# The second half's output projection as seven half-size block products, with the row scales moved into the left factors

## The chip, the cores and the metric

One core of a Trainium2 chip runs the kernel. The metric is the device time of one execution in microseconds (us). Everything is float32; a product is made of three fast passes, by splitting each operand into a high and a low part (high x high, high x low, low x high).

## What is computed

```python
proj = einsum('bld,de->ble', rms_norm(x, norm_w), w_in)        # 2048 tokens, 2048 -> 4608
q, k, v, z_attn, u, z_ssm = split(proj, ...)
o_attn = swa_sink_attention(q, k, v, positions, ...) * silu(z_attn)    # 1024 wide
y = gelu(s5_ssm(u, ...))
y = y * sigmoid(y @ w_glu + b_glu)
o_ssm = y * silu(z_ssm)                                          # 1024 wide
merged = concatenate([rms_norm(o_attn, attn_out_norm_w), rms_norm(o_ssm, ssm_out_norm_w)])
out = x + einsum('ble,ed->bld', merged, w_out)                   # 2048 -> 2048
```

## The kernel before, in words

The 2048 tokens go in two halves of 1024. What one stage leaves for another goes through buffers in HBM (OA for the attention's output, YS for the ssm's, ZS and ZA for the gates). A list scheduler orders the instructions of each engine from the program's order and from priorities; steps of a side task get a priority 800 instructions ahead of their place. Each engine, and SyncE's queue (SP), which issues the DMAs, then works through its own queue in that order.

At the end of the program stand three stages. First the *panels* of the first half's output: `out_panel` makes 256 columns for 1024 tokens with the two row groups of `w_out` one after the other (i = 0, 1). Each group takes 192 matmuls of `panel_tok` (L343) into four PSUM banks (psg, of which there are four), 384 a panel. As a group ends, VectorE (DVE) scales it by row and adds it into four tiles xr that hold x. `weave` runs seven of these panels beside `attend_all`, the second half's attention: 16 groups of four heads and two query blocks, 64 *pairs* of two heads and one block. A pair is four score matmuls (L516), a masked softmax on DVE and ScalarE (ACT), two transposes (L541), the split of the probabilities (ph, pl), their masking (pm: the high part on GpSimd (POOL), the low part on DVE) and four value matmuls (L556). `self.stage` hands out the 512 KB staging tiles (pool stg, four buffers, tag "s"): the four xr of a panel are such tiles, and so is whatever else is loaded for a while.

Then `glu`: eight panels of `panel_feat` (L325) for the gated unit, with `tail_attn` as its side task. It loads the attention rows (oa, a staging tile), splits them with the gain into mh/ml (`split`), and sums their squares into acca; `row_scale` makes the row factors ra from it. At its end the ssm rows yg are split too, and rss is made.

Last `out_wide`: the second half's output, 512 columns at a time over all eight banks, 2 x 8 weight tiles of 128x512 for each. `w_unit` loads a tile (wr), ACT copies it to wh, DVE makes wl = wr - wh, and 24 matmuls (L979) use it. Three buffers each hold wr, wh and wl. The row factors ra and rss come in as the banks are emptied.

## Time and profile before

| | before |
|---|---|
| three runs | 2889.68, 2891.08, 2891.10 us (median 2891.08) |
| profiled execution, its span | 2892.7 us |
| granted TensorE clock, mean | 0.992 |
| TensorE (PE) busy | 2813.6 us, 97% |
| DVE busy | 1900.9 us, 66% |
| ACT busy | 968.2 us, 33% |
| POOL busy | 201.0 us, 7% |

The span runs from the first to the last instruction of one profiled execution. PE is the engine to watch: what another engine does costs time only where PE waits for it. A share over the whole span mixes stages with different limits, so the rows further down are taken by stretches of time.

### The profile page before, as it was taken

Reading aid. Unit: us, or ns where it says so; the run is one execution under the profiler, and the core shown is the slowest. Engines: PE = TensorE matmul, PEld = TensorE weight load, DVE = VectorE, ACT = ScalarE, POOL = GpSimd, SP = SyncE. Lnnn points to the kernel's source line nnn. Section 1 sums busy time; section 2 is a strip of 40 time slices with the busy share of each in tenths; the row PEclk is TensorE's granted clock in tenths of the full one; section 3 lists DMA queues with packets and bytes.
Section 4 is the critical chain, followed back from the end, with each engine's and each line's share of the span. In section 5 each row is a group of like instructions: output and inputs, shape, how many; then the busy total and the mean of one; then the engine's idle time right before and its main releaser. Section 6 shows DMA issues by size and latency. Waiting matters only on the chain.

```text
span 2892.7 us, 45678 instructions
## 1 busy us (share of the span) xinstructions
PE 2813.6 (97%) x17123; PEld 2515.5 (87%) x17123; DVE 1900.9 (66%) x4479; ACT 968.2 (33%) x2117; POOL 201.0 (7%) x341
## 2 busy tenths in 40 slices
PE   6899999989999999999999999998999999899999
PEld 5789999878888888888999988878999999778887
DVE  6681746856773776677779985378999875842222
ACT  6421212133442444333323332255444433521110
POOL 0000000001110021100000000000222220000000
PEclk9999999999999999999999999999999999999999
DMA  5842526553332533445455554343444436333321
GB/s 175 226 123 63 164 88 172 142 141 106 99 113 76 177 108 97 128 145 146 146 160 151 149 154 141 116 125 95 144 135 124 125 111 189 99 101 107 106 78 58
DMA packets 430541, 369.09 MB, mean 128 GB/s; under 512 B 56560, under 2 KB 388848, under 8 KB 430320
## 3 DMA queue, kind: packets, MB, share of 16 engines
q1 hardware_dynamic: 428256, 366.16, 42.6%
q8 instruction: 135, 2.21, 0.3%
q14 instruction: 86, 0.70, 0.1%
q10 hardware_dynamic: 2064, 0.01, 0.0%
HBM read 270.74 MB, written 99.55 MB: 128 GB/s over the span
## 4 chain that ended last, share of the span: by engine, by line
PE 81%; DVE 8%; DMA 7%; SPq 2%; ACT 1%; issue 1%; POOL 0%; ACTq 0%; POOLq 0%; DVEq 0%
PE psg L325 32%; PE psg L343 28%; PE psg L979 6%; PE pss L979 3%; DMA oa<-OA 2%; PE pss L516 2%; PE pso L556 2%; PE pso L979 1%; PE pst L979 1%; DVE ml L93 1%; DMA xst<-in_x_dram 1%; DVE yg L84 1%; PE pst L541 1%; DMA TCS<-St 1%; PE pss L810 1%
## 5 line engine op out<-in xcount | busy, mean ns | idle before, releaser
L84 DVE TENSOR_TENSOR wl<-wr,wh 128x512 fp32r<-128x512 f32 x456 | 315.4, 692 | 544.2 <-ACT wh L311 534.7
L311 ACT CAST wh<-wr 128x512 fp32r<-128x512 f32 x456 | 283.2, 622 | 1007.8 <-PE psg L325 330.9
L325 PE MATMUL psg<-xh,wl 128*128 128x512 f32 x1536 | 495.0, 394 | 7.2 <-DVE wl L84 7.2
L325 PE MATMUL psg<-xl,wh 128*128 128x512 f32 x1536 | 498.4, 395 | 0.0
L325 PE MATMUL psg<-xh,wh 128*128 128x512 f32 x1536 | 493.9, 395 | 0.5 <-ACT xh L235 0.5
L343 PE MATMUL psg<-wl,xh 128*128 128x256 f32 x1536 | 435.2, 284 | 0.0
L343 PE MATMUL psg<-wh,xh 128*128 128x256 f32 x1536 | 434.2, 284 | 1.0 <-ACT rx L389 1.0
L343 PE MATMUL psg<-wh,xl 128*128 128x256 f32 x1536 | 434.2, 284 | 0.0
L325 PEld LDWEIGHTS psg<-xh,wl 128*128 128x128 f32 x1536 | 287.8, 189 | 65.2 <-DVE wl L84 8.9
L325 PEld LDWEIGHTS psg<-xh,wh 128*128 128x128 f32 x1536 | 287.0, 189 | 57.2 <-ACT xh L235 0.9
L325 PEld LDWEIGHTS psg<-xl,wh 128*128 128x128 f32 x1536 | 288.1, 189 | 55.8
L343 PE MATMUL psg<-wh,mh 128*128 128x256 f32 x1024 | 289.9, 286 | 8.6 <-ACT tt L927 7.8
L343 PEld LDWEIGHTS psg<-wh,xh 128*128 128x128 f32 x1536 | 293.6, 192 | 1.4 <-ACT rx L389 1.2
L343 PEld LDWEIGHTS psg<-wl,xh 128*128 128x128 f32 x1536 | 294.2, 192 | 0.4 <-DVE wl L84 0.2
L343 PEld LDWEIGHTS psg<-wh,xl 128*128 128x128 f32 x1536 | 293.7, 192 | 0.0
L343 PE MATMUL psg<-wl,mh 128*128 128x256 f32 x1024 | 290.2, 285 | 0.6 <-DVE wl L84 0.6
L343 PE MATMUL psg<-wh,ml 128*128 128x256 f32 x1024 | 288.9, 285 | 0.0
L84 POOL TENSOR_TENSOR pm<-ph,sel 128x256 fp32r<-128x256 f32 x240 | 189.5, 811 | 983.1 <-ACT ph L544 647.2
L343 PEld LDWEIGHTS psg<-wh,mh 128*128 128x128 f32 x1024 | 195.1, 192 | 9.4 <-ACT tt L927 8.0
L343 PEld LDWEIGHTS psg<-wl,mh 128*128 128x128 f32 x1024 | 196.4, 192 | 0.8 <-DVE wl L84 0.8
L343 PEld LDWEIGHTS psg<-wh,ml 128*128 128x128 f32 x1024 | 195.4, 192 | 0.0
L533 ACT ACTIVATE sm<-pss,mx,rs 128x128 f32<-128x128 f32 x240 | 108.6, 459 | 96.3 <-DVE mx L93 90.5
(419 smaller groups left out, 4663.0 us busy)
## 6 DMA issues: line engine op xcount, KB each, us to landing
wr<-in_w_in_dram SPq DMA_DIRECT2D x296, 256.0 KB
wr<-in_w_out_dram SPq DMA_DIRECT2D x128, 256.0 KB
tb<-TCS SPq DMA_DIRECT2D x64, 256.0 KB
xr<-in_x_dram SPq DMA_DIRECT2D x64, 256.0 KB
out_dram<-xr SPq DMA_DIRECT2D x64, 256.0 KB
raw<-MBC SPq DMA_DIRECT2D x32, 384.0 KB
kst<-KK SPq DMA_DIRECT2D x56, 192.0 KB
xst<-in_x_dram SPq DMA_DIRECT2D x16, 512.0 KB
```

What stands on the lines that cost most here:

```text
L84: (eng or self.nc.vector).tensor_tensor(out=out, in0=a, in1=b, op=op)
L93: self.nc.vector.scalar_tensor_tensor(out=out, in0=a, scalar=s, in1=b, op0=op0, op1=op1)
L311: nc.scalar.copy(hi, raw)
L325: nc.tensor.matmul(ps[t], wt[:, kk, :], xx[k][:, t * 512:(t + 1) * 512], start=(k == 0 and i == 0), stop=(k == nkc - 1 and i == 2))
L343: nc.tensor.matmul(o, xx[k][:, sl], wt[:, kk, :], start=(k == 0 and i == 0 and t % 2 == 0), stop=(k == nkc - 1 and i == 2), skip_group_che ...
L516: nc.tensor.matmul(ps[:, h * 256:h * 256 + 256], qst[:, bq % 2, hp * 2 + h, :], kst[:, i, ksl], start=(h == 0 and i == 0), stop=(i == 1), ...
L533: nc.scalar.activation(sm[:, h, :], sc[:, h, :], AF.Exp, scale=rs[:, h:h + 1], bias=negm[:, h:h + 1], accum_out=den[:, h:h + 1])
L541: nc.tensor.transpose(pt[:, h * P:(h + 1) * P], sm[:, h, :], self.ident)
L556: nc.tensor.matmul(po, vst[:, blk + kb, :], pm[:, i, kb], start=(i == 0 and kb == 0), stop=(i == 1 and kb == 1))
L810: nc.tensor.matmul(o, m[:, g, 0:128], u[:, g, 384:640], start=(g == 0 and i == 0), stop=(i == 2), skip_group_check=True)
L979: nc.tensor.matmul(ps[t], xx[k0 + k][:, t * P:(t + 1) * P], wt[:, 0, :], start=(k == 0 and j == 0), stop=(k == 7 and j == 2))
```

## The change

The second half's projection Y = A W is cut into 2 x 2 blocks: A by tokens (2 x 512) and by rows (attention, ssm), W by rows and by columns (B11, B12, B21, B22 of 1024 x 1024). Instead of eight block products it makes seven, of sums and differences of the blocks (Strassen). The row factors can't then wait for the eviction: `spread` turns ra and rss into full tiles rba and rbs, and the left factors are scaled before they are combined. The attention's sum of squares is made earlier, as nine more steps behind the attention's 33 in the weave with the panels (`attn_stats`, in place of that part of `tail_attn`). The left factors stand in three slots (fh, fl) and are formed by side tasks: slots 0 and 1 beside the gated unit (`form_first`), the others each beside an earlier product. Combinations of weight blocks are made on POOL from two loaded tiles; two of them (T3, T2) are also stored to HBM for a later product. A product is two column halves of eight steps; a step is one weight tile and 12 matmuls into four banks. `final` adds x and a base on POOL and the bank on DVE.

```diff
+    def attn_stats(self, half, pool):
+        nc = self.nc
+        acc = pool.tile([P, HT], F32, tag="acca", name="acca")
+        hs = slice(half * HT, half * HT + HT)
+        for m in range(8):
+            o = self.stage("oa")
+            self.ld.dma_start(o, self.OA[m * P:(m + 1) * P, hs])
+            if m == 0:
+                nc.scalar.activation(acc, o, AF.Square)
+            else:
+                nc.scalar.activation(o, o, AF.Square)
+                self.tt(acc, acc, o, ALU.add, nc.gpsimd)
+            yield
+        self.ra = self.row_scale(pool, acc, 1.0, "ra")
+        yield
...
+    def spread(self, r, out, pool):
+        nc = self.nc
+        for q in range(2):
+            ps = self.psa()
+            for j in range(4):
+                dg = pool.tile([P, P], F32, tag="diag", name="diag", bufs=2)
+                self.ts(dg, self.ident, r[:, q * 4 + j:q * 4 + j + 1], ALU.mult)
+                nc.tensor.matmul(ps[:, j * P:(j + 1) * P], self.ones, dg, start=True, stop=True)
+            nc.scalar.copy(out[:, q * 512:(q + 1) * 512], ps)
...
+    def attn_scaled(self, k, t0, n):
+        o = self.stage("ob")[:, 0:n]
+        self.ld.dma_start(o, self.OA[k * P:(k + 1) * P, HT + t0:HT + t0 + n])
+        self.stt(o, o, self.aow[:, k:k + 1], self.rba[:, t0:t0 + n], ALU.mult, ALU.mult)
+        return o
+    def form_first(self):
+        for k in range(8):
+            o = self.attn_scaled(k, 0, HT)
+            self.split_to(0, k, o[:, 0:512])
+            self.tt(o[:, 512:HT], o[:, 0:512], o[:, 512:HT], ALU.subtract, self.nc.gpsimd)
+            self.split_to(1, k, o[:, 512:HT])
+            yield
+    def ssm_view(self, k, j):
+        return self.yg[k].rearrange("p (t c) -> p t c", t=8)[:, :, j * 64:j * 64 + 64]
+    def form_ssm(self):
+        for k in range(8):
+            y = self.yg[k].rearrange("p (t c) -> p t c", t=8)
+            self.stt(y, y, self.sow[:, k:k + 1], self.rbs.rearrange("p (c t) -> p t c", t=8), ALU.mult, ALU.mult)
+            self.split_to(2, k, self.ssm_view(k, 0), perm=True)
+            yield
+    def form_s2(self):
+        f = lambda x: x.rearrange("p (c t) -> p t c", t=8)
+        for k in range(8):
+            o = self.attn_scaled(k, 0, HT)
+            a1, a2 = o[:, 0:512], o[:, 512:HT]
+            self.tt(a1, a2, a1, ALU.subtract, self.nc.gpsimd)
+            self.tt(f(a1), f(a1), self.ssm_view(k, 1), ALU.add)
+            self.split_to(0, k, a1)
+            v = self.ssm_view(k, 0)
+            self.tt(v, v, f(a1), ALU.subtract)
+            yield
+    def form_s1(self):
+        f = lambda x: x.rearrange("p (c t) -> p t c", t=8)
+        for k in range(8):
+            a2 = self.attn_scaled(k, 512, 512)
+            self.tt(f(a2), f(a2), self.ssm_view(k, 1), ALU.add)
+            self.split_to(1, k, a2)
+            yield
+    def form_view(self, i, j):
+        for k in range(8):
+            self.split_to(i, k, self.ssm_view(k, j), perm=True)
+            yield
...
+    def product(self, slot, first, second, save, evac, side, steps):
+        nc = self.nc
+        step = 0
+        for n in range(2):
+            ps = [self.psg() if n == 0 else self.psa() for t in range(4)]
+            for k in range(8):
+                raw = self.w_load(first, k, n)
+                if second is not None:
+                    q, op = second
+                    r2 = self.w_load(q, k, n, True)
+                    self.tt(raw, raw, r2, op, nc.gpsimd)
+                    if save is not None:
+                        self.st.dma_start(save[k, n], raw)
+                hi = self.wp.tile([P, 1, 512], F32R, tag="wh", name="wh")[:, 0]
+                lo = self.wp.tile([P, 1, 512], F32R, tag="wl", name="wl")[:, 0]
+                nc.scalar.copy(hi, raw)
+                self.tt(lo, raw, hi.bitcast(F32), ALU.subtract)
+                c, o = 4 * slot + k // 2, (k % 2) * 512
+                for t in range(4):
+                    sl = slice(o + t * P, o + t * P + P)
+                    for j, (xx, wt) in enumerate(((self.sh[c], hi), (self.sh[c], lo), (self.sl[c], hi))):
+                        nc.tensor.matmul(ps[t], xx[:, sl], wt, start=(k == 0 and j == 0), stop=(k == 7 and j == 2))
+                step += 1
+                if step * steps // 16 > (step - 1) * steps // 16:
+                    with self.tc.high_priority(offset=_PRIO[2]):
+                        next(side, None)
+            for t in range(4):
+                evac(n, t, ps[t])
+        for _ in side:
+            pass
+    def strassen_out(self, pool):
+        nc = self.nc
+        dt = lambda n: self.dr.tile([8, 2, P, 512], F32, tag=n, name=n)
+        T3, T2 = dt("T3"), dt("T2")
...
+        def e1(n, t, ps):
+            nc.scalar.copy(e(n, t), ps)
+        def e7(n, t, ps):
+            self.tt(v(n, t), e(n, t), ps, ALU.add)
+        def e2(n, t, ps):
+            final(0, 0, n, t, ps, e(n, t))
+        def e6(n, t, ps):
+            self.tt(e(n, t), e(n, t), ps, ALU.add)
+            self.tt(v(n, t), v(n, t), ps, ALU.add)
+        def e5(n, t, ps):
+            self.tt(e(n, t), e(n, t), ps, ALU.add)
+            final(1, 1, n, t, ps, v(n, t))
+        def e3(n, t, ps):
+            final(0, 1, n, t, ps, e(n, t))
+        def e4(n, t, ps):
+            final(1, 0, n, t, ps, v(n, t), ALU.subtract)
+        def ssm_side():
+            self.rss = self.row_scale(pool, self.gacc, 0.125, "rs")
+            self.spread(self.rss, self.rbs, pool)
+            yield
+            yield from self.form_ssm()
+        B11, B12, B21, B22 = 0, 1, 2, 3
+        self.product(0, B11, None, None, e1, ssm_side(), 9)
+        self.product(1, B22, (B12, ALU.subtract), T3, e7, self.form_s2(), 8)
+        self.product(2, B21, None, None, e2, self.form_s1(), 8)
+        self.product(0, B11, (T3, ALU.add), T2, e6, self.form_view(2, 0), 8)
+        self.product(1, B12, (B11, ALU.subtract), None, e5, self.form_view(0, 1), 8)
+        self.product(2, B22, None, None, e3, iter(()), 0)
+        self.product(0, T2, (B21, ALU.subtract), None, e4, iter(()), 0)
...
         for _ in side:
             pass
+        if half:
+            self.yg, self.gacc = yg, acc
+            return
         for m in range(8):
             self.split(k0 + m, yg[m], self.sow[:, m:m + 1], True)
...
-    def out_wide(self, n):
-        """512 columns of the second half's result, with all eight banks."""
-        nc = self.nc
-        for i, k0 in enumerate((0, 8)):
-            ps = [self.psg() if t < 4 else self.psa() for t in range(8)]
-            for k in range(8):
-                hi, lo = self.w_unit(self.a["w_out"], i * 1024 + k * P, 1, n * 512, 512)
-                for t in range(8):
-                    for j, (xx, wt) in enumerate(((self.xh, hi), (self.xh, lo), (self.xl, hi))):
-                        nc.tensor.matmul(ps[t], xx[k0 + k][:, t * P:(t + 1) * P], wt[:, 0, :],
-                                         start=(k == 0 and j == 0), stop=(k == 7 and j == 2))
...
         o0 = O(0)
         with tc.tile_pool(name="at1", bufs=1) as pool:
-            self.weave(o0[:-1], self.attend_all(pool, 1), 33, 0.0, 0.5, PA)
+            def at_side():
+                yield from self.attend_all(pool, 1)
+                yield from self.attn_stats(1, pool)
+            self.weave(o0[:-1], at_side(), 42, 0.0, 0.7, PA)
         with tc.tile_pool(name="tl1", bufs=1) as pool:
+            self.sh, self.sl = [None] * 16, [None] * 16
+            self.rba = pool.tile([P, HT], F32, tag="rba", name="rba")
+            self.rbs = pool.tile([P, HT], F32, tag="rbs", name="rbs")
             yin = self.glu_in(1, pool, 8)
+            self.spread(self.ra, self.rba, pool)
             self.weave(o0[-1:])
-            self.glu(1, pool, yin, self.tail_attn(1, pool, 0), 8)
-        self.rab[1] = (self.ra, self.rss)
-        with tc.tile_pool(name="ox", bufs=1) as self.oxp:
-            for n in range(4):
-                for _ in self.out_wide(n):
-                    pass
+            self.glu(1, pool, yin, self.form_first(), 8)
+            with tc.tile_pool(name="wq", bufs=1) as self.wq:
+                self.strassen_out(pool)
```

Three places of the order in which the instructions stand. In these rows L-numbers are of the kernel named, out<-in are tiles, and x4 a count.

**PE, after 1728 of the 3072 panel matmuls (4.5 panels).** L343 is a panel's matmul (psg, mh, ml), L486 a transpose of q, L516 scores, L541 transposes of probabilities, L556 values. Before:
```order
L343 MATMUL psg<-wh,mh_19884 128x256
L556 MATMUL pso<-pm,vst 128x256 x4
L343 MATMUL psg<-wl,mh_19884 128x256
L343 MATMUL psg<-wh,ml_19885 128x256
L343 MATMUL psg<-wh,mh_19916 128x256
L343 MATMUL psg<-wl,mh_19916 128x256
L343 MATMUL psg<-wh,ml_19917 128x256
L343 MATMUL psg<-wh,mh_19916 128x256
L343 MATMUL psg<-wl,mh_19916 128x256
```
Now, at the same place:
```order
L343 MATMUL psg<-wl,mh_19884 128x256
L343 MATMUL psg<-wh,ml_19885 128x256
L556 MATMUL pso<-pm,vst 128x256 x4
L486 MATMUL pst<-ident,q_22899 128x128 x4
L556 MATMUL pso<-pm,vst 128x256 x4
L516 MATMUL pss<-kst,qst 128x256 x4
L541 MATMUL pst<-ident,sm 128x128 x2
L516 MATMUL pss<-kst,qst 128x256 x4
L556 MATMUL pso<-pm,vst 128x256
L541 MATMUL pst<-ident,sm 128x128 x2
```
The next panel matmul (mh_19916, the second row group of the fifth panel) has moved behind all that is left of the attention: 104 value matmuls, 80 score matmuls, 48 and 20 transposes stand in between.

**SP, the DMA queue, at the end of the attention in the changed kernel.** OA<-oT stores attention output, oa<-OA loads a staging tile for the statistics, xr<-in_x_dram loads the fifth panel's x (also staging tiles), wr loads weights.
```order
L570 DMA OA<-oT 128x2x256
L478 DMA vst<-VS 128x3x128
L482 DMA zT<-ZA 128x2x256
L570 DMA OA<-oT 128x2x256 x3
L909 DMA oa<-OA 128x1024
L1184 DMA xr<-in_x_dram 128x2x256 x4
L308 DMA wr<-in_w_out_dram 128x2x256 x3
L1189 DMA out_dram<-xr 128x2x256 x3
L909 DMA oa<-OA 128x1024
```
Before, the fifth panel's xr stand in this queue right behind the stores of the fourth panel's, with attention still to come; now four oa come there, and xr has moved behind the last stores of the attention and the seventh oa.

**DVE, in the first of the seven products, eleventh to twelfth weight tile (wl).** diag and rbs belong to `spread`, yg are the ssm rows.
```order
L84 TENSOR_TENSOR wl<-wr,wh 128x512
L88 TENSOR_SCALAR diag<-ident,rsr 128x128 x4
L93 SCALAR_TENSOR_TENSOR yg_26179<-yg_26179,sow,rbs 128x1024
L93 SCALAR_TENSOR_TENSOR yg_26185<-yg_26185,sow,rbs 128x1024
L93 SCALAR_TENSOR_TENSOR yg_26191<-yg_26191,sow,rbs 128x1024
L93 SCALAR_TENSOR_TENSOR yg_26197<-yg_26197,sow,rbs 128x1024
L93 SCALAR_TENSOR_TENSOR yg_26203<-yg_26203,sow,rbs 128x1024
L93 SCALAR_TENSOR_TENSOR yg_26209<-yg_26209,sow,rbs 128x1024
L93 SCALAR_TENSOR_TENSOR yg_26215<-yg_26215,sow,rbs 128x1024
L93 SCALAR_TENSOR_TENSOR yg_26221<-yg_26221,sow,rbs 128x1024
L84 TENSOR_TENSOR ob<-ob,yg_26179 128x8x64
L84 TENSOR_TENSOR wl<-wr,wh 128x512
```
Before, the ssm rows were split at this place with weight tiles between them:
```order
L84 TENSOR_TENSOR wl<-wr,wh 128x512
L93 SCALAR_TENSOR_TENSOR ml_27367<-yg_26139,sow,mh_27366 128x4x128
L84 TENSOR_TENSOR yg_26157<-yg_26157,sz 128x512
L93 SCALAR_TENSOR_TENSOR ml_27367<-yg_26139,sow,mh_27366 128x4x128
L93 SCALAR_TENSOR_TENSOR ml_27373<-yg_26145,sow,mh_27372 128x4x128 x2
L93 SCALAR_TENSOR_TENSOR ml_27379<-yg_26151,sow,mh_27378 128x4x128 x2
L93 SCALAR_TENSOR_TENSOR ml_27385<-yg_26157,sow,mh_27384 128x4x128
L84 TENSOR_TENSOR accs<-accs,tt 128x4x128
```
All eight scalings have moved in front of the twelfth wl, and each is over 1024 elements. Up to the fifteenth wl there follow 14 strided and 6 plain operations (three of them wl), up to the fourth wl of the second product 8 strided, 4 of 128x1024 and 9 plain, and from there to its ninth 5 strided and 10 plain (five of them wl).

## Rows read from the trace of the kernel before

**Rows 1.** The page's first line and section 1: busy time of each engine, share, instructions
```profile
span 2892.7 us, 45678 instructions
...
PE 2813.6 (97%) x17123; PEld 2515.5 (87%) x17123; DVE 1900.9 (66%) x4479; ACT 968.2 (33%) x2117; POOL 201.0 (7%) x341
```

**Rows 2.** Windows: busy us (x instructions) of PE, PEld, DVE, ACT, POOL; clock, DMA
```profile
2017.00:2241.00 224.00, 223.18 (x1881) 222.71 (x1881) 207.86 (x642) 100.86 (x336) 64.10 (x80) 1.00 0.44 132
2241.00:2370.00 129.00, 128.99 (x1088) 128.75 (x1087) 116.18 (x349) 53.15 (x175) 37.27 (x48) 1.00 0.38 116
```

**Rows 3.** Windows, panel matmuls of line L343 alone: busy us (x) of PE, PEld
```profile
2241.00:2370.00 129.00, 114.43 (x848) 106.06 (x847) 1.00 0.38 116
2370.00:2428.00 58.00, 57.69 (x482) 57.59 (x481) 1.00 0.55 159
```

**Rows 4.** Windows, the attention's value matmuls of line L556 alone
```profile
2241.00:2370.00 129.00, 17.90 (x96) 14.19 (x96) 1.00 0.38 116
2370.00:2428.00 58.00, 0.64 (x4) 0.55 (x4) 1.00 0.55 159
```

**Rows 5.** Window, instructions on tile wl: busy us (x) of PE, PEld, DVE
```profile
2241.00:2370.00 129.00, 79.61 (x282) 53.43 (x282) 12.30 (x18) 1.00 0.38 116
```

**Rows 6.** Window, instructions on tile xr: busy us (x) of DVE
```profile
2241.00:2370.00 129.00, 14.02 (x33) 1.00 0.38 116
```

**Rows 7.** Waits of PE from 2380 us on: us in total, times, longest
```profile
PE psg L979 <- ACT wh L311: 3.9, 1, 3.9
PE pst L979 <- DVE ram L90: 2.0, 1, 2.0
PE pss L860 <- DVE accs L84: 1.3, 1, 1.3
PE psg L979 <- DVE wl L84: 1.3, 1, 1.3
```

**Rows 8.** Pieces of the chain in order of time: start us, us, what
```profile
2454.58 3.95 DMA oa<-OA
...
2464.15 5.50 DMA oa<-OA
...
2562.01 2.72 PE psg L979 x12
...
2883.69 5.51 DVE xr L93 x8
```

**Rows 9.** A window at the transition, columns as in rows 2
```profile
2530.00:2540.00 10.00, 4.07 (x11) 2.49 (x10) 10.00 (x13) 5.35 (x7) 0.00 (x0) 0.72 0.08 19
```

**Rows 10.** Groups by line from 2400 us on: xcount, busy us, mean ns, idle before
```profile
L84 DVE TENSOR_TENSOR wl<-wr,wh 128x512 fp32r<-128x512 f32 x84 | 57.9, 689 | 225.0 <-ACT wh L311 225.0
L311 ACT CAST wh<-wr 128x512 fp32r<-128x512 f32 x84 | 52.2, 622 | 310.4 <-PE pss L979 285.8 <-PE psg L343 24.5
...
L84 DVE TENSOR_TENSOR yg<-yg,sz 128x512 f32<-128x512 f32 x16 | 18.5, 1154 | 0.1
...
L84 DVE TENSOR_TENSOR acca<-acca,oa 128x1024 f32<-128x1024 f32 x7 | 8.6, 1222 | 1.4 <-ACT oa L897 1.3
```

**Rows 11.** Timeline of DVE: start us, us, what, xcount
```profile
2040.59 0.42 DVE L84 TENSOR_TENSOR sm<-sm,mx 128x256 f32<-128x256 f32 x1
...
2042.85 0.75 DVE L84 TENSOR_TENSOR pm<-pl,sel 128x256 fp32r<-128x256 f32 x2
...
2045.56 0.41 DVE L84 TENSOR_TENSOR pl<-pst,ph 128x256 fp32r<-128x256 f32 x1
2045.88 0.72 DVE L84 TENSOR_TENSOR sm<-sm,mx 128x256 f32<-128x256 f32 x1
2046.53 1.30 DVE L84 TENSOR_TENSOR pm<-pl,sel 128x256 fp32r<-128x256 f32 x2
```

**Rows 12.** Timeline of POOL in the same stretch
```profile
2045.58 1.63 POOL L84 TENSOR_TENSOR pm<-ph,sel 128x256 fp32r<-128x256 f32 x2 [2.67 <-ACT ph L544]
```

**Rows 13.** Groups by line of POOL over the span
```profile
L84 POOL TENSOR_TENSOR pm<-ph,sel 128x256 fp32r<-128x256 f32 x240 | 189.5, 811 | 983.1 <-ACT ph L544 647.2 <-ACT mx L535 241.1 <-issue 76.2
```

More of the change, by code (lines that the diff above doesn't have):

```diff
@@ new lines, in strassen_out, with part, rows, final @@
+    def strassen_out(self, pool):
+        nc = self.nc
+        dt = lambda n: self.dr.tile([8, 2, P, 512], F32, tag=n, name=n)
+        T3, T2 = dt("T3"), dt("T2")
+        acc = {}
+        def part(n, c, t):
+            i = (8 * c + 4 * n + t) // 2
+            if i not in acc:
+                acc[i] = self.xt.tile([P, HT], F32, tag=f"x{'hl'[i // 4]}{12 + i % 4}", name=f"ac{i}")
+            return acc[i][:, (t % 2) * 512:(t % 2) * 512 + 512]
+        e = lambda n, t: part(n, 0, t)
+        v = lambda n, t: part(n, 1, t)
+        def rows(y, r, c, n, t):
+            r0 = HT + r * 512 + t * P
+            return y[0, r0:r0 + 2 * P, c * 1024 + n * 512:c * 1024 + n * 512 + 512].rearrange("(t p) c -> p t c", p=P)
+        xs = {}
+        def final(r, c, n, t, ps, base, op=ALU.add):
+            if t % 2 == 0:
+                x = xs[0] = self.stage("xr").rearrange("p (t c) -> p t c", t=2)
+                self.ld.dma_start(x, rows(self.a["x"], r, c, n, t))
+            x = xs[0]
+            o = x[:, t % 2]
+            self.tt(o, o, base, ALU.add, nc.gpsimd)
+            self.tt(o, o, ps, op)
+            if t % 2:
+                self.st.dma_start(rows(self.out, r, c, n, t - 1), x)
+        def e1(n, t, ps):
[27 more added lines that the diff above has]
+        self.product(0, T2, (B21, ALU.subtract), None, e4, iter(()), 0)
```

40 lines of the change are left out of this document (28 added, 12 removed).

## The prediction

> **What bounds the kernel now.** I read the page first, then windows of the second half, engine by engine and line by line, then the waits and the chain in time. TensorE (PE) is busy 97% of the span [rows 1]; wherever it stays busy, time falls only with fewer matmuls. Two stretches matter. From 2017 to 2428 us the panels of the first half's output (L343) are woven with the second half's attention. PE has no hole there, and VectorE (DVE) is close behind: 116.2 of 129 us between 2241 and 2370 [rows 2]. Attention reaches almost to the end of the panels: 96 of its value matmuls (L556, four to a pair of heads and a query block) stand between 2241 and 2370 and only 4 behind [rows 4], while 848 + 482 panel matmuls come after 2241 [rows 3]. From about 2527 us on the final projection (L979) runs without a hole at 2.72 us for each weight tile of 12 matmuls [rows 8]. Between the two, the gated unit ends in a transition where PE waits 3.9 + 2.0 + 1.3 + 1.3 us [rows 7] and its granted clock falls to 0.72 for a while [rows 9].
>
> **The part that the words of the change name: the products.** L979 has 4 x 2 x 8 x 8 x 3 = 1536 matmuls, the seven products have 7 x 2 x 8 x 4 x 3 = 1344, in steps of 12. 192 fewer at 2.72 / 12 = 0.227 us is **-43.5 us**. The long wait for the ssm split at the transition goes, because the first product (P1) needs attention rows alone, formed beside the gated unit: 8.5 us of waits plus about 2 of half clock, so **-10** (between -6 and -12, since P1 may wait for banks). The end is shorter: four evictions instead of eight, half of 5.5 us [rows 8], **-3**.
>
> What is added stands on DVE, in the queue that also makes the low half of every weight tile (wl). Costs from [rows 10]: wl 0.69, a strided 128x512 1.15, a plain 128x1024 1.22. Back to back each starts about 0.09 before the last one's end (two of 0.42 take 0.75 [rows 11]), so they cost 0.60, 1.07 and 1.13. A 128x1024 with a strided operand has no row; between 1.13 and twice 1.15 I take 2.15, since the strided rows cost almost twice the plain ones. The order of DVE gives four holes, each the DVE sum between two wl less what PE still has:
> - The eleventh wl of P1 is followed by eight scalings of the ssm rows (L93 yg<-yg,sow,rbs) and an addition ahead of the twelfth. They wait for rbs, whose last ones-matmuls stand in PE's queue after step 10.25, so DVE can't begin early. 8 x 2.15 + 1.07 + 0.7, and 0.7 for ACT's copy (0.62 [rows 10]), is 19.7; PE has 2.0 us left of its step. 17.6, or 9.4 with the low price.
> - To the fifteenth wl: 14 strided and 6 plain operations, 18.6, and one GpSimd (POOL) combination; PE has three steps, 8.2. 11.
> - To the fourth wl of P2: 18.5 of DVE against five steps, 13.6. On top come loads of the attention rows (a 512 KB load took 4.0 to 5.5 us [rows 8]) that wait for stage tiles just set free, and eight POOL operations. 5 to 20, I take 13.
> - To the ninth: 11.3 of DVE and five POOL operations against 13.6. 0 to 5, I take 4.5.
>
> Why POOL counts on DVE's time: beside a POOL pair of 1.63 us [rows 12], DVE's sm took 0.72 where 0.42 is usual, and the pair of pm 1.30 where 0.75 is usual [rows 11]. These read two SBUF operands; pl<-pst, which reads PSUM, kept its 0.41 [rows 11]. A POOL 128x256 takes 0.81 [rows 13], so a 128x512 lies between 0.8 and 1.6; I take 1.4 and let it add in full. The Trainium skill (SBUF — State Buffer, section "SBUF: two separate sides") says that the two engines share one port pair as an exclusive lock when a DVE operation has two SBUF inputs and the GpSimd one reads SBUF. By that rule, the trace agreeing in direction, the holes come to the 46 below; if the engines ran beside each other they would come to about 28.
>
> Sum of the holes: 17.6 + 11 + 13 + 4.5 = **+46** (25 to 56). From there to P7 DVE and POOL together take about what PE takes; for the products that store a combined weight tile (P2, P4), whose load buffer then also waits for the store, and for P5 and P7, where POOL both combines weights and adds bases, I allow **+5** (0 to 30). The projection thus comes to -43.5 - 10 - 3 + 46 + 5 = **-5**: its saving is spent on DVE.
>
> **The part that the words do not name: the attention's statistics.** They move from the gated unit into the weave of attention and panels, and their 512 KB loads (oa) take stage tiles, of which there are four; a panel's four xr tiles come from the same four. In the queues the loads for the fifth panel's xr stand behind the oa load of m = 6, whose rows are those of the last four heads: complete only when attention is. Without xr the fifth panel can't empty its four banks, and PE can't go on. PE's queue says the same: after panel matmul 1728 come 104 value matmuls, 80 score matmuls and 48 transposes, 20 to 26 pairs, without one panel matmul; then the other 1344, with no attention. The 1728th ran at about 2241 us before.
>
> So a stretch in which PE had two kinds of work falls in two. Alone, 25 pairs go at DVE's pace or slower. Between 2241 and 2370 DVE spent 116.2 - 12.3 - 14.0 = 89.9 us on 24 pairs, wl and xr taken off [rows 2, 5, 6]: 3.75 each, the floor. The pace then was 129 / 24 = 5.4, the ceiling if everything else keeps it. DVE was 90% busy, so 3.75 / 0.9 = 4.2, nearer the floor; POOL's additions of 128x1024 (up to four times 0.81) in the same queue as its pm add a little: 4.3, hence 107 us. Then the last attention rows are stored (no row; 0 to 4, I take 2.5), m = 6 is loaded (about 4.5 [rows 8]), squared (about 1, less than two of ACT's 0.62 [rows 10]), added on POOL (3), and the last xr load follows (3, less than the 512 KB row): 14. The 1344 panel matmuls take 58 / 482 = 0.120 us each at most [rows 3], 160 us. Row-scale matmuls that need m = 7 stand some 280 panel matmuls later and wait about 4, and PE restarts at a lower clock for some 2. Before, all that took 2428 - 2241 = 187. 107 + 14 + 160 + 6 - 187 = **+100** (with 94, 6 and 0: +73; with 135, 17 and 8: +133).
>
> The gated unit I leave at nothing: beside each of its panels DVE still has one 128x1024 and two 128x512 to form the attention rows, and POOL one subtraction more; -5 to +6.
>
> **Sum.** 2892.7 + 100 - 5 = 2987.7 in the profiled execution, whose span lies 1.6 us above the median of the runs shown, 2891.1. Predicted: **2986 us**.
>
> **The rivals.**
> - *The chain, not DVE, sets the pace of the lone attention.* PE has only about (129 - 848 x 0.120) / 24 = 1.1 us a pair, a quarter of the stretch, so its clock may fall as at the transition [rows 9]; scores, transposes and value matmuls then take longer, and with single banks for transposes and values little overlaps. At 5.2 to 5.6 a pair: 25 to 30 more, about 3013. For it: before, these chains were hidden by panels and nobody saw them. Against it: DVE's row is nearly full at 90%.
> - *The weight tiles bound the products.* P2 loads two tiles and stores one a step, beside 4 MB of attention rows; each of three load buffers waits for two landings and POOL. At 3.5 us a step over 32 steps: 25 more, about 3010.
> - *Everything at its cheap end.* 94 a stretch, holes of 25 to 30: about 2945.
> - *Faster: PE passes the waiting attention.* If PE's queue could run panel matmuls ahead of the stalled attention, +100 would vanish and -5 stand, 2886; it decides for faster as soon as the stretch costs under 0. Against it: the panel's banks would still be full, because xr is missing, and 25 pairs of 3.75 us of DVE fit nowhere else.
>
> **How the numbers follow.** My forecast, 2955 to 3000, has 0.52; the chain 0.2; the weight tiles 0.12; the cheap end 0.12; faster 0.03; no change 0.01. Leaving out the faster case and the outer parts of the others gives 2938 to 3038. A measurement here tells about 0.2% (6 us) from nothing. Slower 0.95, same 0.02, faster 0.03.
>
> **What would show it.** Attention: a stretch of about 105 us from 2241 without L343, PE a quarter to a third busy, DVE above 85%, then a hole of some 14 us, panels ending near 2528 instead of 2428. Projection: 1344 matmuls of the new line at 2.72 a step, with PE holes of some 18, 11 and 13 us before the twelfth and fifteenth steps of P1 and the fourth of P2, DVE full in them, and POOL operations lengthening DVE's two-SBUF ones. I am wrong if panels run on through the attention, if DVE is not full while PE waits, or if the strided 128x1024 costs near 1.2.

## The result, and the profile after

| | before | changed |
|---|---|---|
| median of four runs each, same chip | 2890.38 us | 3046.51 us (3040.76 to 3056.81) |
| ratio to before, 95% interval | | 1.0546 [1.0532, 1.0559] |
| profiled execution, its span | 2892.7 us | 3055.1 us |
| granted TensorE clock, mean | 0.992 | 0.963 |

156 us slower, where 95 were predicted; the time lies 8 us above the range. The profiled execution of the changed kernel is the longest of its four, 10 us above their median, so its spans add up to 162 us.

First the page of the changed kernel, which answers to [rows 1]. GpSimd's (POOL's) busy time has doubled, and DVE has 155 us more.
```profile
span 3055.1 us, 46107 instructions
...
PE 2848.4 (93%) x16963; PEld 2520.9 (83%) x16963; DVE 2056.4 (67%) x4616; ACT 1020.9 (33%) x2201; POOL 399.3 (13%) x460
```
Then the windows of the attention that stands alone, of the hole behind it and of the panels that follow (columns as in [rows 2]), and the panel matmuls alone (PE, PEld):
```profile
2246.00:2347.00 101.00, 66.07 (x245) 50.69 (x244) 96.62 (x300) 48.07 (x161) 41.44 (x50) 0.55 0.23 72
2347.00:2357.00 10.00, 0.13 (x1) 0.00 (x0) 1.98 (x5) 1.44 (x2) 0.33 (x1) 0.50 0.51 155
2357.00:2524.00 167.00, 166.79 (x1375) 166.59 (x1376) 56.51 (x115) 26.77 (x38) 4.44 (x2) 0.99 0.39 114
...
2246.00:2357.00 111.00, 0.00 (x0) 0.00 (x0) 0.54 0.25 79
2357.00:2524.00 167.00, 164.45 (x1343) 163.36 (x1344) 0.99 0.39 114
```
Of the 111 us without a panel matmul, DVE is busy in 96.6 of the first 101, and PE runs at half its clock. The pieces of the chain behind the attention are its store and one load of x (start us, us, what):
```profile
2345.94 1.21 PE pso L556 x4
...
2348.97 2.12 DMA OA<-oT
...
2351.70 4.55 DMA xr<-in_x_dram
...
2356.28 0.89 DVE xr L93 x2
```
PE's waits from 2380 us on, which answer to [rows 7]:
```profile
PE psg L1043 <- ACT wh L1037: 26.0, 11, 10.6
PE pso L1043 <- DVE wl L84: 18.2, 3, 14.5
PE pso L1043 <- ACT wh L1037: 15.2, 7, 6.9
PE psg L1043 <- DVE wl L84: 13.8, 8, 4.6
PE psg L325 <- ACT tt L1149: 12.5, 4, 5.9
PE psg L1043 <- ACT tt L1149: 4.5, 2, 3.8
PE pss L1043 <- ACT rbs L928: 0.7, 1, 0.7
```
Without the gated unit (L325) these are 78.4 us. Windows of the seven products, P1 to P7 in order:
```profile
2629.20:2718.70 89.50, 57.15 (x226) 44.69 (x225) 62.58 (x77) 27.65 (x40) 16.95 (x3) 0.81 0.25 73
2718.70:2787.30 68.60, 53.19 (x194) 39.52 (x193) 51.10 (x49) 16.06 (x28) 36.65 (x23) 0.88 0.75 227
2787.30:2834.70 47.40, 45.59 (x193) 36.84 (x192) 31.14 (x42) 18.23 (x26) 9.05 (x6) 0.96 0.60 184
2834.70:2896.40 61.70, 48.68 (x194) 35.91 (x192) 31.66 (x36) 17.88 (x24) 31.26 (x21) 0.97 0.71 226
2896.40:2957.80 61.40, 49.11 (x193) 38.39 (x194) 29.54 (x37) 12.63 (x19) 32.66 (x23) 0.92 0.59 180
2957.80:3001.30 43.50, 43.50 (x194) 36.02 (x193) 20.42 (x31) 9.97 (x16) 15.23 (x11) 1.00 0.66 205
3001.30:3050.40 49.10, 45.30 (x193) 35.38 (x191) 17.09 (x24) 8.69 (x14) 23.37 (x18) 1.00 0.63 193
sum 421.20, PE 342.52 PEld 266.74 DVE 243.53 ACT 111.11 POOL 165.18; mean PE 48.93 PEld 38.11 DVE 34.79 ACT 15.87 POOL 23.60
```
P6, which neither combines nor forms anything, takes 43.5 us: the price of 192 matmuls. Seven of these are 304.5 us, so the products lose 421.2 - 304.5 = 117: 78 in which PE stands, and 342.5 - 304.5 = 38 in which it works longer. One reason is seen behind the longest hole (PE's timeline, then the window behind it):
```profile
2674.95 0.39 PE L1043 MATMUL pss<-wh,fh 128*128 128x512 f32 x1
2689.87 0.79 PE L1043 MATMUL pso<-wl,fh 128*128 128x512 f32 x1 [14.54 <-DVE wl L84]
2690.47 0.63 PE L1043 MATMUL pso<-wh,fl 128*128 128x512 f32 x1
2690.89 0.63 PE L1043 MATMUL pss<-wl,fh 128*128 128x512 f32 x1
...
2690.00:2696.00 6.00, 6.00 (x14) 4.66 (x15) 6.00 (x8) 1.46 (x3) 0.00 (x0) 0.50 0.48 118
```
Matmuls that otherwise start every 0.23 us start every 0.43 for the next 6 us, at a granted clock of 0.50 (the lower of its two levels, 1.2 GHz). The seven longest waits are each followed by such a stretch, which costs some 1 to 3 us more. Most of the others aren't: P7 has three waits, a clock of 1.00 throughout, and PE is still 1.8 us longer at work there than in P6.

Counted in PE's timeline of all seven products, 83 matmuls start 0.43 us apart; with the slow first ones behind the waits that is some 19 of the 38 us. Some 3 are 32 small matmuls of `row_scale` and `spread`. The other 16 stand at the waits themselves: a matmul's record lasts 0.39 us where the next usually starts after 0.23, so that each wait adds 0.16 to the busy time; the first matmul behind a wait takes 0.34 to the next; and waits of less than 0.16 are hidden in busy time.

The sum by stages, in the profiled executions: the panels end at 2524.4 us (before 2428.6), +96; the gated unit takes 104.8 instead of 96.2, +9; from the first matmul of the projection to the end it is 425.9 instead of 367.9, +58. A few us of that can be this one execution's: late_stats below has the same products, and in its trace they take 414.7 us instead of 421.2.

### The profile page after: what moved, and what is told of

It reads as the page before. It is cut to its first block, busy times and chain, and to the rows that moved or that the text cites. A ratio compares the mean times of both kernels' runs of the same rounds, so it can differ in the third digit from the quotient of the medians.

```text
span 3055.1 us, 46107 instructions
## 1 busy us (share of the span) xinstructions
PE 2848.4 (93%) x16963; PEld 2520.9 (83%) x16963; DVE 2056.4 (67%) x4616; ACT 1020.9 (33%) x2201; POOL 399.3 (13%) x460
## 4 chain that ended last, share of the span: by engine, by line
PE 69%; DVE 12%; DMA 11%; issue 3%; POOL 2%; SPq 2%; ACT 2%; POOLq 0%; DVEq 0%; ACTq 0%
PE psg L325 30%; PE psg L343 27%; DMA wr<-in_w_out_dram 2%; PE psg L1043 2%; PE pss L516 2%; POOL wr L84 2%; DMA ob<-OA 2%; PE pso L556 1%; DMA oa<-OA 1%; DVE wl L84 1%; DVE yg L84 1%; DMA wr<-T 1%; PE pst L541 1%; DMA TCS<-St 1%; DVE yg L93 1%
## 5 line engine op out<-in xcount | busy, mean ns | idle before, releaser
L84 DVE TENSOR_TENSOR wl<-wr,wh 128x512 fp32r<-128x512 f32 x504 | 369.2, 734 | 545.0 <-ACT wh L311 386.8
L311 ACT CAST wh<-wr 128x512 fp32r<-128x512 f32 x392 | 242.6, 620 | 818.1 <-PE psg L325 341.9
L325 PE MATMUL psg<-xl,wh 128*128 128x512 f32 x1536 | 498.7, 396 | 0.0
L325 PE MATMUL psg<-xh,wl 128*128 128x512 f32 x1536 | 495.0, 394 | 3.3 <-DVE wl L84 3.3
L325 PE MATMUL psg<-xh,wh 128*128 128x512 f32 x1536 | 494.0, 395 | 1.1 <-ACT wh L311 0.6
L343 PE MATMUL psg<-wh,xh 128*128 128x256 f32 x1536 | 435.0, 284 | 1.9 <-ACT rx L389 1.9
L343 PE MATMUL psg<-wl,xh 128*128 128x256 f32 x1536 | 435.8, 284 | 0.0
L343 PE MATMUL psg<-wh,xl 128*128 128x256 f32 x1536 | 434.7, 284 | 0.0
L325 PEld LDWEIGHTS psg<-xh,wl 128*128 128x128 f32 x1536 | 288.1, 189 | 61.1 <-DVE wl L84 4.4
L325 PEld LDWEIGHTS psg<-xh,wh 128*128 128x128 f32 x1536 | 287.0, 189 | 57.9 <-ACT wh L311 1.0
L325 PEld LDWEIGHTS psg<-xl,wh 128*128 128x128 f32 x1536 | 288.2, 189 | 56.0
L343 PE MATMUL psg<-wh,mh 128*128 128x256 f32 x1024 | 291.2, 287 | 18.6 <-DVE xr L93 10.8
L343 PEld LDWEIGHTS psg<-wh,xh 128*128 128x128 f32 x1536 | 294.4, 192 | 2.2 <-ACT rx L389 2.1
L343 PEld LDWEIGHTS psg<-wl,xh 128*128 128x128 f32 x1536 | 295.0, 192 | 0.1
L343 PEld LDWEIGHTS psg<-wh,xl 128*128 128x128 f32 x1536 | 294.4, 192 | 0.0
L343 PE MATMUL psg<-wl,mh 128*128 128x256 f32 x1024 | 290.7, 285 | 0.6 <-DVE wl L84 0.6
L343 PE MATMUL psg<-wh,ml 128*128 128x256 f32 x1024 | 288.8, 285 | 0.0
L343 PEld LDWEIGHTS psg<-wh,mh 128*128 128x128 f32 x1024 | 196.7, 193 | 19.8 <-DVE xr L93 11.8
L343 PEld LDWEIGHTS psg<-wl,mh 128*128 128x128 f32 x1024 | 197.9, 193 | 0.8 <-DVE wl L84 0.8
L343 PEld LDWEIGHTS psg<-wh,ml 128*128 128x128 f32 x1024 | 196.3, 193 | 0.0
L1037 ACT CAST wh<-wr 128x512 fp32r<-128x512 f32 x112 | 69.4, 623 | 250.9 <-POOL wr L84 179.8
```

The source lines that it names most:

```text
L84: (eng or self.nc.vector).tensor_tensor(out=out, in0=a, in1=b, op=op)
L311: nc.scalar.copy(hi, raw)
L325: nc.tensor.matmul(ps[t], wt[:, kk, :], xx[k][:, t * 512:(t + 1) * 512], start=(k == 0 and i == 0), stop=(k == nkc - 1 and i == 2))
L343: nc.tensor.matmul(o, xx[k][:, sl], wt[:, kk, :], start=(k == 0 and i == 0 and t % 2 == 0), stop=(k == nkc - 1 and i == 2), skip_group_che ...
L1037: nc.scalar.copy(hi, raw)
```

## The experiments

Each kernel was timed four times (late_spread_deep seven, late_spread_deep2 eleven), with before on the same chip, whose medians there lay between 2889.7 and 2892.0 us; the three tests of the two engines ran once. Differences are to the changed kernel's 3046.5 unless said. The times of P1 to P7 come from one trace each. late_stats and the changed kernel have the same products; their traces agree within 1 us in each of them but P4, which takes 56.6 and 61.7 us. A difference of 5 us in P4 alone therefore says nothing.

**late_stats** undoes the move of the statistics:
```diff
-            self.weave(o0[:-1], at_side(), 42, 0.0, 0.7, PA)
+            self.weave(o0[:-1], self.attend_all(pool, 1), 33, 0.0, 0.5, PA)
+            for _ in self.attn_stats(1, pool):
+                pass
```


> The attention's statistics no longer stand in the weave: they follow it, ahead of the eighth panel; everything else is as in the changed kernel. Theory (staging tiles): the 112 us without panel matmuls exist only because the fifth panel's x waits behind a statistics load; they vanish and panels and attention run beside each other again: 96 us less than the changed kernel, about 2950, up to 10 more if the gated unit waits for the row factors. Rival (the extra work on ACT and GpSimd, or the longer weave, slows the attention itself): less than half comes back, 3000 or more.


Measured: 2970.2 us, -76, ratio 1.0280 [1.0263, 1.0297]. Its windows of all engines from 2241 to 2370, and of the panel matmuls, are those of [rows 2, 3] again:
```profile
2241.00:2370.00 129.00, 129.00 (x1088) 128.76 (x1087) 116.68 (x351) 53.40 (x174) 37.19 (x48) 1.00 0.38 116
...
2241.00:2370.00 129.00, 114.75 (x848) 106.31 (x848) 1.00 0.38 116
```
The panels end at 2434.3, 90 us earlier than in the changed kernel's trace. The theory holds for the cause; by the medians 76 came back, not 96. The two traces differ by 3055.1 - 2963.1 = 92 us; the changed kernel's is of its longest execution, 10 above its median, and that of late_stats of its shortest, 5 below.

**dve_comb**, `self.tt(raw, raw, r2, op)` without `nc.gpsimd`, makes the combinations on DVE.


> The weight combinations are made on DVE instead of GpSimd. Theory (loads): P4, P5 and P7 wait for a loop of load, combination and next load through two r2 buffers and one in-order DMA queue; a combination of 0.7 instead of 1.3 us shortens that loop a little: P4 and P5 together 5 to 10 us less, the 10.6 us hole before the last steps of P1 falls to about 4, P2 gains DVE work; in all 10 to 20 less than the changed kernel, about 3030. Rival (the two engines exclude each other, and that alone stretches the products): P4, P5, P7 fall to about 47 us each and the hole goes: 35 to 45 less, about 3005.


Measured: 3031.1, -15. P4 56.5, P5 53.8, P7 47.6 us, the 10.6 us hole 7.9. The sum is the first theory's; P5 gained more than it said, and P4 has what late_stats shows with the combinations on GpSimd.

**r2x3**, `bufs=3` for r2 and `bufs=1` for diag:


> Three buffers instead of two for the second weight tile of a combination (the diag tile gets one buffer instead of two to make room). Theory (loads): a third load can be under way, so the loop over load and combination no longer sets the pace: P4 and P5 from 61 to about 53 us, P7 from 49 to 46, in all 15 to 22 less than the changed kernel, about 3028. Rival (GpSimd and DVE excluding each other): 0 to 3 less.


Measured: 3050.2, +4: no gain in the whole. P3 took 43.5 us instead of 47.4, but P1 92.7 and P2 71.2; P4 56.9 and P5 60.7 are what late_stats has.

**nostore** hands `product` no place to save to, so that `self.st.dma_start(save[k, n], raw)` isn't reached:


> The combined tiles T3 and T2 are not stored; P4 and P7 load a block of w_out in their place (so P4 and P7 multiply by other combinations than they should). Theory (loads, with the stores in the same in-order queue): loads no longer stand behind stores that wait for GpSimd, and a load buffer is free without a store: P2 3 to 6 us less, P4 8 to 12 less, P5 and P7 as they were; in all 12 to 18 less, about 3031. Rival (GpSimd and DVE excluding each other): 0 to 3 less.


Measured: 3050.4, +4. P2 70.9, P4 54.9, P5 60.5. As I had put it, as a matter of one r2 buffer or of the stores, the theory of the loads falls.

**plain_scale** writes rbs in the order of the rows, and reads it so (cut to these lines):
```diff
-            nc.scalar.copy(out[:, q * 512:(q + 1) * 512], ps)
+            if perm:
+                nc.scalar.copy(out.rearrange("p (t c) -> p c t", t=8)[:, q * 64:q * 64 + 64, :], ps.rearrange("p (c t) -> p c t", t=8))
+            else:
+                nc.scalar.copy(out[:, q * 512:(q + 1) * 512], ps)
...
-            self.stt(y, y, self.sow[:, k:k + 1], self.rbs.rearrange("p (c t) -> p t c", t=8), ALU.mult, ALU.mult)
+            self.stt(y, y, self.sow[:, k:k + 1], self.rbs, ALU.mult, ALU.mult)
```


> The row factors rbs are spread in the order in which the ssm rows lie, so that the eight scalings in P1 read plain rows; all else is as in the changed kernel. Theory (length of the burst): each scaling falls from 2.02 to about 1.2 us, the 14.5 us hole to 8, and the total falls by 6 to 10 us, to about 3038. Rival (the time of the burst is set by the sum that waits behind it, GpSimd included): the hole is shorter, the next one longer, 0 to 3 less.


Measured: 3045.5, -1; 6 us in P1 of its trace (the hole 8.0 instead of 14.5) that the medians don't show. Inconclusive: the executions of either kernel differ by as much.

**spread** leaves all operations and ties each to its step (cut):
```diff
+        self.nc.scalar.activation(g, self.hi[:, 0:1].bitcast(F32), AF.Identity, scale=0.0, bias=col)
...
+        for g, at in ((ssm_side(), [0, 11, 13, 15, 17, 19, 21, 23, 25]), (self.form_s2(), range(24, 48, 3)),
+                      (self.form_s1(), range(48, 64, 2)), (self.form_view(2, 0), range(64, 80, 2)),
+                      (self.form_view(0, 1), range(80, 96, 2))):
```


> The same operations as in the changed kernel, but the side tasks are spread out: each scaling takes its gain through a small ACT copy that reads a weight tile of the step to which it belongs, so that it can't be moved ahead; the ssm rows are formed from the twelfth step of P1 to the tenth of P2, the rows for P4 over P2 and P3, those for P5 in P4, the last two groups in P5 and P6. Theory (bursts in DVE's queue): the 14.5 and 10.6 us holes of P1 and those of P2 go, with the half clock behind them: P1 from 89.5 to about 60, P2 from 68.6 to about 50, P4 and P5 hardly changed; 40 to 55 less than the changed kernel, about 3000. Rival (the sum of DVE's and GpSimd's work sets the pace): the holes move to P2 to P4, and no more than 15 comes back, 3030 or more.


Measured: 3026.0, -20, between the two. Its windows of P1, P3 and P4 (P2 took 64.1 us, not the 50 of the theory):
```profile
2622.30:2673.70 51.40, 48.28 (x225) 39.48 (x224) 30.21 (x50) 19.06 (x32) 6.58 (x2) 1.00 0.34 96
...
2737.80:2797.60 59.80, 48.90 (x193) 38.12 (x193) 47.59 (x53) 20.33 (x34) 27.60 (x16) 0.91 0.52 165
2797.60:2867.30 69.70, 54.34 (x194) 41.00 (x193) 58.60 (x62) 23.92 (x39) 34.38 (x20) 0.85 0.78 245
```
P1 lost 38 us, so its holes were bursts; but 8 to 12 us each came back in P3 and P4, where DVE is now 80 to 84% busy with GpSimd beside it. Both theories have a part.

**late_spread** is late_stats, plain_scale and spread in one.


> Three of the edits together: the attention's statistics after the weave, rbs in the order of the rows, and the side tasks spread out. If bursts are what the products lose, and the edits add up: 2970 from the first, 45 less from the last, 5 less from the middle one, about 2920 (2900 to 2935), still slower than the kernel before. Rival (the sum of the work): 2950 or more.


Measured: 2942.7, ratio 1.0181 [1.0164, 1.0198], between the two. The edits add up as measured (3046.5 - 76 - 1 - 20 = 2949, and 7 less than that), not as expected.

**nocomb** has `None` for every second block and store:


> Leaves out all four combinations of weight blocks with their second loads and the two stores (the products multiply by single blocks of w_out); rows, evictions and bases are as in the changed kernel. Theory (combinations, with the loads and the GpSimd time behind them, stretch P4, P5 and P7): P4, P5 and P7 at 45 to 48 us, P2 at 55 to 60, the 10.6 us hole at the end of P1 at 3 or less; 45 to 60 less than the changed kernel, about 2993. Rival (the evictions with two additions for each bank stretch P4 and P5): P4 and P5 stay at 55 or more, total 3015 or more.


Measured: 2984.3, -62. P2 47.7, P4 43.5, P5 45.4, P7 43.7 us; the hole at the end of P1 2.9 us with another of 3.6. The theory holds: what stretches P2, P4, P5 and P7 comes with the combinations, that is with GpSimd's part, the second loads and the stores together.

**nobase** leaves out `self.tt(o, o, base, ...)` and one addition each in e6 and e5:


> Leaves out the additions of bases (GpSimd's in the final step, and one DVE addition for each bank of P4 and of P5), so that the output lacks those terms; combinations are as in the changed kernel. Theory (combinations): P4 from about 58 to 55, P5 from 60 to 54, P7 from 49 to 47, 8 to 15 less in all, about 3035. Rival (evictions and bases): P4 and P5 fall to 45 to 47, 28 or more less, 3018 or less.


Measured: 3031.5, -15. P4 58.8, P5 51.8, P7 45.2: the theory in the sum, though P5 owes 10 us to its evictions. How, the changed kernel's timeline of GpSimd shows at P5's longest hole (6.85 us, to 2947.21):
```profile
2942.81 2.48 POOL L84 TENSOR_TENSOR xr<-xr,ac 128x512 f32<-128x512 f32 x2 [8.30 <-DMA xr<-in_x_dram]
2945.25 2.49 POOL L84 TENSOR_TENSOR wr<-wr,wr 128x512 f32<-128x512 f32 x2
```
Two additions of a base wait 8.3 us for their x in GpSimd's queue, and the combination that PE needs stands behind them.

**two_engines, two_engines2, two_engines3** measure DVE and GpSimd beside each other.


> This kernel leaves out the whole computation and writes a test tile in place of the result: chains of 24 additions of 128x512 on DVE with five additions on GpSimd beside them, DVE reading two SBUF operands, one SBUF and one PSUM operand, or one SBUF operand, and each alone. Theory (exclusion): alone a GpSimd addition takes about 1.3 us and a DVE one 0.6; beside back-to-back two-operand DVE work a GpSimd addition starts and then stands until DVE pauses, so at least one of the five lasts 5 us or more; beside PSUM or one-operand work all stay near 1.3 us. Rival (they share a rate): beside two-operand work every GpSimd addition takes up to twice as long, 1.5 to 2.6 us, and none more.

> As the first test of the two engines alone (it too leaves out the whole computation), but DVE's 24 operations don't depend on each other, so that each can begin before the last one ends. Theory (GpSimd gets the port only where DVE pauses): beside two-operand DVE work one GpSimd addition of 128x512 lasts until the 24 are through, about 14 us, as the one of 14.0 us in P1 did; beside PSUM or one-operand work 1.3 to 1.8 us each. Rival (they take turns, as with dependent operations): each lasts 1.6 to 1.8 us and costs DVE about 1 us.

> A third test of the two engines alone (the computation is left out, a test tile is written): five GpSimd additions of 128x512 beside 16 DVE operations of two SBUF operands: plain, with strided rows as in the forming of the rows, with strided rows and a rounded result as in fl, and plain with a rounded result as in wl. Theory (strided rows keep the port): beside strided work one GpSimd addition lasts until DVE pauses, 10 us or more; beside plain work 1.7. Rival (turns there too, so that the 14.0 us in P1 have another cause): none lasts over 3 us, and each costs DVE about 1 us.


DVE's timeline of two_engines2 (24 operations of two SBUF operands alone, then beside five GpSimd additions; with one PSUM operand; with one SBUF operand; ahead of them four of one operand alone), and GpSimd's four later additions alone and beside these:
```profile
5.17 1.42 DVE L61 TENSOR_SCALAR dd<-bin 128x512 f32<-128x512 f32 x4
...
15.27 14.53 DVE L64 TENSOR_TENSOR dd<-go,ain 128x512 f32<-128x512 f32 x24
...
31.17 19.86 DVE L64 TENSOR_TENSOR dd<-go,ain 128x512 f32<-128x512 f32 x24
...
52.58 14.44 DVE L67 TENSOR_TENSOR dd<-go,ps 128x512 f32<-128x512 f32 x24
...
68.46 13.46 DVE L70 TENSOR_SCALAR dd<-go 128x512 f32<-128x512 f32 x24
...
8.62 5.28 POOL L73 TENSOR_TENSOR pp<-pp,bin 128x512 f32<-128x512 f32 x4
...
32.45 6.59 POOL L73 TENSOR_TENSOR pp<-pp,bin 128x512 f32<-128x512 f32 x4
...
53.75 5.32 POOL L73 TENSOR_TENSOR pp<-pp,bin 128x512 f32<-128x512 f32 x4
```
In all three the engines took turns: a GpSimd addition takes 1.65 us instead of 1.3 (1.9 to 2.05 beside strided rows), and each costs DVE (19.86 - 14.53) / 5 = 1.07 us; with strided rows 5.38 / 5 = 1.08 (15.85 and 21.23 us for 16 in two_engines3). Beside a PSUM operand neither loses: 1.33 us an addition, and the 24 operations take no more than those of two SBUF operands alone. No addition lasted until DVE paused: the theory fell in all three.

**deep** gives wr five buffers (tiles tt and accs, dead by then), r2 three and diag one:


> Five buffers instead of three for wr from P2 on and three instead of two for r2 (in tiles that are dead by then), all else as in the changed kernel. Theory (buffers: a wr tile is held for landing, combination, copy and subtraction, about 9 to 10 us, so that three give a tile each 3.2 us or more): P4 and P5 from 57 to 61 us to about 48 each, P7 to 45, P2 to 62, 25 to 35 less than the changed kernel, about 3016. Rival (the time of GpSimd and DVE): P4 and P5 stay at 55 or more, 0 to 8 less.


Measured: 3027.3, -19. P2 61.5, P4 53.1, P5 59.0, P7 45.9, P3 44.0. Between the two: the buffers are a part for P2, P4 and P7, not for P5.

**late_spread_dve, late_spread_deep, late_spread_deep2** put together what gave something.


> The late_spread kernel with the combinations and the subtraction of P2's side task on DVE, and the side tasks spread a little differently (rows for P4 formed from the fifth step of P2 on, rows for P5 from the fifth of P3 on). If GpSimd's two-operand work costs DVE its time in full: each of 64 combinations costs the pair 0.6 instead of 1.3, P2, P4 and P5 fall to 50, 52 and 50 us, 25 to 40 less than late_spread, about 2910. Rival (the loads and their wait for buffers set P2 and P4): 0 to 12 less, 2930 or more. In neither case faster than the kernel before.

> The late_spread_dve kernel with the five wr and three r2 buffers. If buffers hold P2 to P5 back: P2 50, P3 48, P4 51, P5 48, about 25 less than late_spread_dve, 2894, level with the kernel before; if the work of DVE does: 0 to 8 less, 2912 or more.

> The late_spread_deep kernel with three edits: four wr and three r2 buffers with two diag tiles again (P1 then 50 instead of 56 us), the rows for P5 formed mostly in P4 instead of from P3 on (P3 down by 5, P4 up by 3), and the subtraction beside the gated unit on DVE instead of GpSimd (3 us less there). Theory (DVE's queue, with GpSimd's work on DVE's account): 5 to 12 less than late_spread_deep, 2889 to 2896, level with the kernel before. Rival (what is left are the waits for loads): 2898 to 2905, still slower.


Measured: 2918.9 (1.0100 [1.0085, 1.0115]), 2900.8 (1.0029 [1.0018, 1.0041]) and 2899.3 us (1.0028 [1.0019, 1.0037]). The first gave 24 where the theory said 25 to 40, with P2, P4 and P5 at 55.4, 62.5 and 53.4 us instead of 50, 52 and 50; the second 18, between its two, though P1 grew from 50.1 to 56.1 us with diag's single buffer (51.9 in the third, with two); the third nothing more, so there its rival stands in number. The trace doesn't show the rival's cause, though: of the 43 us of PE's waits left from the gated unit on, 11.2 are in the gated unit and 28.6 for a wl, and of these 28.6 DVE was at work in all but 1. It was DVE's own queue that was late there, not a load. Of the last one, PE's two longest waits, P4, and the sum of all seven products:
```profile
2703.79:2707.15 3.36, 0.00 (x1) 0.01 (x1) 3.36 (x6) 1.19 (x2) 0.00 (x0) 1.00 1.03 397
2762.29:2766.48 4.19, 0.00 (x1) 0.00 (x1) 4.19 (x5) 1.16 (x2) 1.01 (x1) 0.94 0.25 63
...
2696.00:2755.80 59.80, 48.82 (x194) 38.44 (x193) 54.14 (x74) 22.70 (x36) 5.97 (x4) 0.91 0.82 269
...
sum 357.30, PE 325.16 PEld 261.02 DVE 268.10 ACT 115.29 POOL 58.94; mean PE 46.45 PEld 37.29 DVE 38.30 ACT 16.47 POOL 8.42
```
P4 is the longest, with DVE busy 54.1 of 59.8 us. From the first matmul of the products to the last it is 357.3 us, where the 1536 of before took 363.6 (from 2524.8 to 2888.4 in its trace): 6 us are left of the 43.5. The panels end 10 us later than before and the gated unit takes 103 instead of 96. No version here beats the kernel before.

## Why the prediction was wrong

**The attention's statistics: right.** +100 was predicted (73 to 133), +96 is in the trace, and late_stats shows the cause. Not one panel matmul ran in 111 us. The 25 pairs took 101 / 25 = 4.04 us each (4.3 predicted); DVE's 96.6 us make 3.86 each, the floor of 3.75 and a little, and at 96% busy it set the pace. The chain, my first rival, didn't, though PE ran at half clock. The hole behind was 10 instead of 14 us, because the last x load waited only for its place in SP's queue: it was issued 0.4 us behind the load of m = 6, without its square and sum. The 1344 matmuls took 167 where 160 + 6 stood.

**The gated unit: too cheap.** "-5 to +6" became +9. PE waits 12.5 us there for the bank copies of the tanh (tt). Before, it waited 6.4, a line that [rows 7] leaves out:
```profile
PE psg L325 <- ACT tt L927: 6.4, 4, 2.2
```
That is 6 of the 9; the rest is PE longer at work (92.3 instead of 89.8 us, at a clock of 0.95 instead of 1.00). DVE and GpSimd have the extra operations of the forming; that these are the cause was only argued.

**The projection: this is the step that failed,** -5 (to +30) predicted, +58 measured. By its terms:

| term | predicted | measured |
|---|---|---|
| 192 matmuls fewer | -43.5 | -43.5 (43.5 for P6's 192) |
| holes of P1, P2 and P3 | +46 | 32.4 + 15.4 + 1.8 = +50 |
| P4, P5 and P7 | +5 (0 to 30) | 13.0 + 12.3 + 3.8 = +29 |
| PE longer at work in the products | none | +38 |
| what the transition of before cost | -10 | -15 (363.6 less 1536 x 0.227) |
| the end | -3 | 0 |

The measured holes are a window's length less PE's busy time in it. The terms add up to 58 within rounding. In their sum the holes of P1 to P3 were sized almost rightly, 50 for 46, but in part by luck. The one ahead of the twelfth step has 14.5 us where 17.6 stood, and eight scalings took 16.2 us, 2.02 each, where 2.15 was taken. The one in the fifteenth has 10.6 where 11 stood, but it ended with P2's first combination, on GpSimd; nocomb, without any, has 2.9 and 3.6 there, and dve_comb, with it on DVE, 7.9. Another 7 us of P1 stand in its first steps and at rbs. P2's 15.4 are ten waits of at most 5.3, where one of 13 and one of 4.5 stood. (Without GpSimd the prediction's own numbers give 17.6 + 10.4 + 4.9 = 33, not "about 28".) Two terms were far off.

*What each hole costs PE beside its length was left out.* I counted half clock once, 2 us at the attention's end, and took "about 2" off at the transition of before; [rows 9] had shown 0.72. But the changed kernel has not one transition but some thirty waits of PE in the products (the counts above): some 19 of the 38 us are half clock behind the longer ones, some 16 stand at the start and end of each wait, and only 3 belong to small matmuls. Where the holes go, it goes: P4 of nocomb has none, and 43.5 us.

*P4, P5 and P7 were allowed 5 us, and lost 29 in holes and 13 more in PE's longer work (some 5 of these by the clock).* I had compared sums, "DVE and POOL together take about what PE takes", and sums don't make holes; order does. nocomb shows that the combinations, with their loads and stores, are the cause. No single part of them is: GpSimd (dve_comb), the buffers (deep), the additions at the evictions (nobase) each give a part, the stores and a third r2 alone nothing in the whole. Waits of SP, GpSimd and DVE from 2835 to 2960 us, P4 and P5:
```profile
SPq L1018 <- POOL wr L84: 36.8, 15, 5.6
...
POOL wr L84 <- DMA wr<-in_w_out_dram: 31.0, 12, 6.6
POOL wr L84 <- DMA wr<-T: 16.1, 5, 6.4
POOL xr L84 <- DMA xr<-in_x_dram: 8.3, 1, 8.3
...
DVE wl L84 <- ACT wh L1037: 61.2, 19, 11.3
```
In these 125 us DVE wasn't short of time: it waited 61 us for wh. GpSimd waited 47 for weight loads, whose issue (L1018) waited 37 for GpSimd's combinations: a loop. A combined tile passes two loads, GpSimd, ACT and DVE one behind another, in queues where the evictions and formed rows stand too, and three buffers give it some 8 us of lead (3 x 2.72). The rival "the weight tiles bound the products" was nearest, with 25 us; but it put them on P2 and P4 and on loads and stores, and P5 lost as much with no store.

**That POOL costs DVE its own time: right in size, and an open end.** 1.07 us for a GpSimd addition of 1.3, in the tests. The Trainium skill (SBUF — State Buffer, section "SBUF: two separate sides") calls this an exclusive lock that the one who comes first holds for its whole instruction; turns of whole instructions agree with that, and so does the PSUM operand that pays nothing. But in P1 something harder happened. GpSimd's and DVE's timelines there:
```profile
2697.13 14.00 POOL L84 TENSOR_TENSOR wr<-wr,wr 128x512 f32<-128x512 f32 x1 [45.69 <-DMA wr<-in_w_out_dram]
...
2709.33 0.67 DVE L84 TENSOR_TENSOR fl<-ob,fh 128x512 fp32r<-128x512 f32 x1
2711.81 0.69 DVE L84 TENSOR_TENSOR wl<-wr,wh 128x512 fp32r<-128x512 f32 x1 [1.81 <-ACT wh L1037]
```
The first combination of P2 lasted 14.0 us and ended at 2711.13, 1.13 us (about its own length) after DVE's first pause at 2710.00; the 10.6 us hole ends with it, though without a combination 2.9 and 3.6 us remain there (nocomb). In late_stats it lasted 13.0 and ended 1.12 us after DVE's pause, in plain_scale 14.2 and 1.13 us; the traces of r2x3, nostore, nobase and deep show the same, 14.0 to 14.4 us. So GpSimd was shut out there during a run of 15 DVE operations, and the tests, with runs of 16 and 24, didn't reproduce it. What makes the difference is not settled.

Of the predicted signs of a wrong forecast, two did not come: no panel ran through the attention, and the strided scaling cost 2.0. The third came in part. DVE was at work in 39 of the 50 us of PE's waits in P1 to P3, but only in 10 of the 29 in P4, P5 and P7.

## What to carry to other kernels

Before work is taken off the engine that bounds, write the order of the engine that takes it over, step by step, and look at each point where more stands between two deliveries than the buffers give lead; sums over a stage don't show it. Price each hole of TensorE with what it costs beside its length, here half clock behind the long ones above all, from a row of the same trace. And a load for a side task from a shared ring of tiles can hold up a load of the main work that stands behind it in the same in-order queue: here that one line cost more than all that the change could bring.
